# Feed-forward activations turned by VectorE block transposes and a round trip through memory

## The chip, the core and the metric

One core of a Trainium2 chip runs the whole program. TensorE multiplies matrices (its weight loads, PEld, run beside its matmuls), VectorE (DVE) and ScalarE (ACT) work on tiles element by element, GpSimd (POOL) does a few side tasks, and SyncE (SP) issues nearly all memory transfers; the 16 DMA engines of the core carry them out. The metric is the device time of one execution in microseconds. Three runs of the kernel before gave 1258.07, 1259.29 and 1259.97 us: the median is 1259.29.

## What is computed

One layer of a hybrid trunk over 256 tokens of width 2048, in float32. Two mixers (an RWKV-7 recurrence and a gated delta rule) stand ahead of the part that matters here, the feed-forward:

```python
h = rms_norm(x, ffn_norm_w[l])
x = x + (jax.nn.silu(h @ ffn_w_gate[l]) * (h @ ffn_w_up[l])) @ ffn_w_down[l]
return rms_norm(x, final_norm_w)
```

The hidden width is 5632. All three matrices are read once from memory, 138 MB in float32.

## The kernel before, in words

**Split products.** Every float32 operand is split in two float32r parts, high and low; a product is high x high, low x high and high x low, three matmuls of one pass each. Weights come as loads of 512 KB into `raw` (three buffers); ScalarE copies the high part to `wh` in two halves (line 197) and VectorE subtracts it from `raw` to give `wl` (line 198). `wh` and `wl` have two buffers each. `load_split` (line 172) does this for one load. I call one load and the twelve 512-wide matmuls that it feeds a part.

**The feed-forward** goes over 11 units of 512 hidden columns. For a unit, `gate` and `up` (lines 1071 and 1080, both through `gate_up`, line 1044) each take eight parts, with matmuls at line 1065, and give `sg`, two tiles of 128 tokens x 512 columns: ScalarE takes the silu (line 1076), VectorE multiplies by the `up` product (line 1084). `down` (line 1129) multiplies by `w_dn` in two halves `hf` of four parts each, matmuls at line 1142, and adds into `acc` (line 1150).

**The turn.** `down` needs the activations with hidden columns on partitions, but `sg` has tokens there. `turn` (line 1087) transposes `sg` on TensorE, eight 128x128 transposes (line 1097) into two PSUM banks, and ScalarE and VectorE split these into `h` (lines 241 and 242). The loop (from line 1168) takes the gate of the next unit, the first half of `down` of this one, `up` of the next, and the second half of `down`; in the middle of that half, after its second part, stands the turn of the next unit. The first unit's turn is called straight after its `up`, as there is no `down` before it; the scheduler puts it into the second unit's gate.

**Order.** A scheduler orders each engine's instructions by readiness and priority; loads and splits have high priority, so they run ahead as far as buffers allow. SP issues its transfers strictly in the order given, and each takes the next of eight completion semaphores in turn (DMAHW0 to DMAHW7), so that an issue has to wait until the transfer eight issues before it has landed. In unit 36, the last but one, five loads of the last unit's `w_dn` (`raw_end`, line 1057) stand among the others, through a single buffer; three more were loaded earlier.

Of the kernel before, what the change touches and what calls it, by code (L numbers as in the profile page):

```python
# [9 lines left out]
F32 = mybir.dt.float32  # L10
BF16 = mybir.dt.bfloat16
I32 = mybir.dt.int32
F32R = mybir.dt.float32r
# [4 lines left out]
P = 128  # L18
T = 256
# [30 lines left out]
def trunk_kernel(ctx, tc, xT, vecs, fnw, w_up, a_up, g_up, w_in, w_ab, w_out, w_gu, w_dn, out):  # L50
# [9 lines left out]
    def hi():  # L60
        return tc.high_priority(offset=HI)
# [11 lines left out]
    def mps(name, tag="mr"):  # L73
        return pm.tile([P, 512], F32, tag=tag, name=name)
# [22 lines left out]
    for r in range(2):  # L97
        rows = slice(64 * r, 64 * r + 64)
# [68 lines left out]
            assert any([g.step() for g in list(side)])  # L167


    first = []  # L170

    def load_split(src, by_k=False, whole=False):

        with hi():
            if first:
                raw = first.pop(0)
            else:
                raw = wp.tile([P, 1024], F32, tag="raw", name="raw", bufs=RAW)
                SY.dma_start(out=raw.rearrange("p (c f) -> p c f", c=4) if by_k else raw, in_=src)
            wh = wp.tile([P, 1024], F32R, tag="wh", name="wh", bufs=WH)  # L180
            wl = wp.tile([P, 1024], F32R, tag="wl", name="wl", bufs=WL)
            both = [(wh[:, h * 512:h * 512 + 512], wl[:, h * 512:h * 512 + 512]) for h in range(2)]
            if whole:
                split(wh, wl, raw)
                return both
            it = iter(both)
            return halves_of(raw, lambda: next(it), by_k)
# [856 lines left out]
    def gate_up(c0, m, tag="pb", beside=None):  # L1044

        banks = [pm.tile([P, 512], F32, tag=tag, name="psq") for _ in range(2)]
        b = c0 + 2 * m - NFB + 8
        ends = [(x % 4, x // 4) for x in (b, b + 1, b + 4, b + 5)] if 0 <= b < 4 else []
        for q in range(2):
            for kk in range(4):  # L1050
                if ends and kk % 2:
                    wend[ends[2 * q + kk // 2]] = halves_of(raw, own)
                elif ends:
                    raw = rp.tile([P, 1024], F32, tag="i1", name="raw_end")
                    i_, hf = ends[2 * q + kk // 2]
                    with hi():
                        SY.dma_start(out=raw, in_=w_dn[NFB - 4 + i_, hf])
                parts = load_split(w_gu[c0:c0 + 4, m, q, :, kk * 256:kk * 256 + 256].rearrange("c p f -> p c f"), True)
                for kx in range(2):
                    k = 8 * q + 2 * kk + kx  # L1060
                    t, ri = x2k[k]
                    wh, wl = parts[kx]
                    for o, w in ((0, wh), (T, wh), (0, wl)):
                        for tb in range(2):
                            last = PE.matmul(banks[tb], t[:, ri, o + tb * P:o + tb * P + P], w,  # L1065
                                             start=(k == 0 and o == 0 and w is wh), stop=(k == KB - 1 and w is wl))
                if beside and kk % 2:
                    beside(2 * q + kk // 2, last)
        return banks

    def gate(c0, beside=None):
# [15 lines left out]
    def turn(c0, sg, before=()):  # L1087
# [14 lines left out]
                split(h[:, hs, 0:T], h[:, hs, T:], p3)  # L1102
        return h

    nbank = [0]

    def wend_slots():

        one = ["lw", "SB", "sq2", "bk", "i3"] + ["kt", "rt"] * 2 + ["vt"] * 4
        bufs = {"kt": 2, "rt": 2, "vt": 4}  # L1110

        def places():
            x2w = rp.tile([P, 8, 512], F32R, tag="AT1", name="wend")
            for i in range(8):
                yield x2w[:, i, :]
            w = act.tile([P, 4, 2 * T], F32R, tag="act", name="wend")
            for i in range(4):
                yield w[:, i, :]
            w = rp.tile([P, 2, 512], F32R, tag="Yt", name="wend")
            yield w[:, 0, :]  # L1120
            yield w[:, 1, :]
            for t in one:
                yield rp.tile([P, 512], F32R, tag=t, name="wend", bufs=bufs.get(t, 1))
            for i in range(6):
                yield fp.tile([P, 512], F32R, tag=("wend", "sq2")[i // 4], name="wend", bufs=(4, 2)[i // 4])
        g = places()
        return lambda: (next(g), next(g))
# [26 lines left out]

    def turn_x2(i, before):

        tb, ps = i // 2, [mps("ps_xn", t) for t in ("mr", "mc")]
        q0 = i % 2 * 2
        ms = [PE.transpose(ps[q][:, k * P:k * P + P], x2[:, 4 * (q0 + q) + k, tb * P:tb * P + P], ident)
              for q in range(2) for k in range(4)]  # L1160
        together([before] + ms)
        for q in range(2):
            S.copy(acc[:, tb, (q0 + q) * 512:(q0 + q) * 512 + 512], ps[q])

    sg = gate(units[0], turn_x2)
    h = turn(units[0], up(units[0], sg, "mg"))

    for c, c1 in zip(units, units[1:]):
        sg = gate(c1)
        down(c, h, 0)  # L1170
        up(c1, sg)
        ahead = []
        down(c, h, 1, lambda m: ahead.append(turn(c1, sg, [m])))
        h = ahead[0]


    n = 4
# [110 lines left out]
```

## Time and profile before

| | |
|---|---|
| median of three runs | 1259.29 us |
| profiled execution, its own time | 1257.04 us |
| its span | 1255.3 us |
| TensorE clock granted | 0.998 |
| TensorE busy | 1231.5 us |
| VectorE / ScalarE busy | 835.0 / 650.4 us |
| transposes at line 1097 | 88, 11.4 us in all |
| bytes moved | 226.68 MB, 175701 packets, 181 GB/s |

In the page's groups, a line gives the source line, the engine, what is written from what, the count, the busy time in us and the mean in ns, and behind the second bar the idle time just before these instructions and what ended it. The chain is the sequence of work that ended last, each piece with its start and length. In timelines, a bracket gives the idle time before a piece and what released it.

### The profile page before, as it was taken

Reading aid. Unit: us, or ns where it says so; the run is one execution under the profiler, and the core shown is the slowest. Engines: PE = TensorE matmul, PEld = TensorE weight load, DVE = VectorE, ACT = ScalarE, POOL = GpSimd, SP = SyncE. Lnnn points to the kernel's source line nnn. Section 1 sums busy time; section 2 is a strip of 40 time slices with the busy share of each in tenths; the row PEclk is TensorE's granted clock in tenths of the full one; section 3 lists DMA queues with packets and bytes.
Section 4 is the critical chain, followed back from the end, with each engine's and each line's share of the span. In section 5 each row is a group of like instructions: output and inputs, shape, how many; then the busy total and the mean of one; then the engine's idle time right before and its main releaser. Section 6 shows DMA issues by size and latency. Waiting matters only on the chain.

```text
span 1255.3 us, 21107 instructions
## 1 busy us (share of the span) xinstructions
PE 1231.5 (98%) x8122; PEld 1084.1 (86%) x8122; DVE 835.0 (67%) x1634; ACT 650.4 (52%) x1199; POOL 17.0 (1%) x63
## 2 busy tenths in 40 slices
PE   7999999999999999999999999999999999999997
PEld 6999999999999989888888888888888888878886
DVE  7987887978966867555556555655656565665554
ACT  6665555666545556664444444444444444454443
POOL 3000000000000000000000000000000000000000
PEclk9999999999999999999999999999999999999999
DMA  6555666575573445676666666766666766676651
GB/s 232 167 168 178 162 170 157 168 183 142 179 231 118 135 165 188 167 209 191 190 191 195 188 190 194 197 188 197 186 187 189 194 187 195 202 239 192 194 150 67
DMA packets 175701, 226.68 MB, mean 181 GB/s; under 512 B 52272, under 2 KB 144560, under 8 KB 175344
## 3 DMA queue, kind: packets, MB, share of 16 engines
q1 hardware_dynamic: 171328, 222.19, 60.7%
q10 hardware_dynamic: 4128, 2.10, 0.6%
q8 instruction: 64, 1.05, 0.4%
q0 software_dynamic: 144, 1.05, 0.2%
q14 instruction: 37, 0.30, 0.1%
HBM read 218.75 MB, written 4.46 MB: 178 GB/s over the span
## 4 chain that ended last, share of the span: by engine, by line
PE 86%; DMA 5%; DVE 5%; ACT 1%; SPq 1%; issue 1%; DVEq 0%; ACTq 0%
PE psq L1065 36%; PE psd L1142 17%; PE psb L215 16%; PE psb L218 8%; DMA raw_end<-in_w_dn 2%; DVE wl L242 1%; PE psT L1097 1%; DMA raw<-in_w_in 1%; DMA A_r<-sA 1%; DMA sA<-AT 1%; PE psd L1193 1%; PE psd L1191 1%; PE psd L1192 1%; PE ps_A L480 1%; DVE wend L198 1%
## 5 line engine op out<-in xcount | busy, mean ns | idle before, releaser
L198 DVE TENSOR_TENSOR wl<-raw,wh 128x512 fp32r<-128x512 f32 x524 | 341.5, 694 | 273.0 <-ACT wh L197 271.0
L197 ACT ACTIVATE wh<-raw 128x512 fp32r<-128x512 f32 x524 | 302.0, 625 | 363.2 <-PE psq L1065 203.9
L1065 PE MATMUL psq<-wh,x2s 128*128 128x512 f32 x1408 | 377.4, 390 | 0.4 <-ACT wh L197 0.4
L1065 PEld LDWEIGHTS psq<-wh,x2s 128*128 128x128 f32 x1408 | 263.7, 188 | 55.6 <-ACT wh L197 1.0
L1065 PE MATMUL psq<-wl,x2s 128*128 128x512 f32 x704 | 217.2, 389 | 0.0
L215 PE MATMUL psb<-xs,wh 128*128 128x256 f32 x816 | 207.3, 288 | 7.6 <-ACT wh L197 6.1
L218 PE MATMUL psb<-xs,wh 128*128 128x256 f32 x816 | 206.9, 287 | 0.0
L1142 PE MATMUL psd<-wh,h 128*128 128x512 f32 x640 | 203.5, 391 | 1.0 <-ACT wh L197 1.0
L241 ACT ACTIVATE wh<-raw 128x1024 fp32r<-128x1024 f32 x128 | 135.3, 1057 | 86.6 <-PE psb L218 71.2
L215 PEld LDWEIGHTS psb<-xs,wh 128*128 128x128 f32 x816 | 157.3, 193 | 9.1 <-ACT wh L197 6.1
L242 DVE TENSOR_TENSOR wl<-raw,wh 128x1024 fp32r<-128x1024 f32 x128 | 155.9, 1218 | 10.8 <-ACT wh L241 10.7
L218 PEld LDWEIGHTS psb<-xs,wh 128*128 128x128 f32 x816 | 157.4, 193 | 1.5 <-issue 0.7
L1065 PEld LDWEIGHTS psq<-wl,x2s 128*128 128x128 f32 x704 | 132.0, 188 | 27.5
L1142 PEld LDWEIGHTS psd<-wh,h 128*128 128x128 f32 x640 | 119.1, 188 | 26.3 <-ACT wh L197 2.3
L215 PE MATMUL psb<-xs,wl 128*128 128x256 f32 x816 | 127.8, 287 | 2.2 <-DVE wl L198 1.2
L1142 PE MATMUL psd<-wl,h 128*128 128x512 f32 x320 | 124.6, 389 | 0.0
L215 PEld LDWEIGHTS psb<-xs,wl 128*128 128x128 f32 x816 | 110.4, 193 | 4.5 <-DVE wl L198 2.0
L1142 PEld LDWEIGHTS psd<-wl,h 128*128 128x128 f32 x320 | 60.1, 188 | 12.7
L218 PE MATMUL psb<-ys,wh 128*128 128x256 f32 x256 | 64.5, 288 | 2.5 <-DVE ys L242 2.5
L215 PE MATMUL psb<-ys,wh 128*128 128x256 f32 x256 | 64.7, 289 | 0.2 <-ACT ys L241 0.2
L218 PEld LDWEIGHTS psb<-ys,wh 128*128 128x128 f32 x256 | 50.1, 196 | 2.8 <-DVE ys L242 2.7
L1150 DVE TENSOR_TENSOR acc<-acc,psd 128x512 f32<-128x512 f32 x80 | 49.5, 681 | 1.8 <-PE psd L1142 1.8
(312 smaller groups left out, 1014.2 us busy)
## 6 DMA issues: line engine op xcount, KB each, us to landing
raw<-in_w_gu SPq DMA_DIRECT2D x176, 512.0 KB, 4.8
raw<-in_w_in SPq DMA_DIRECT2D x99, 512.0 KB, 3.9
raw<-in_w_dn SPq DMA_DIRECT2D x80, 512.0 KB, 4.2
raw<-in_w_out SPq DMA_DIRECT2D x32, 512.0 KB, 3.5
raw_end<-in_w_dn SPq DMA_DIRECT2D x8, 512.0 KB, 4.4
xraw<-in_xT SPq DMA_DIRECT2D x8, 256.0 KB, 6.3
x<-in_xT SPq DMA_DIRECT2D x1, 2048.0 KB, 9.7
raw<-in_w_ab SPq DMA_DIRECT2D x2, 512.0 KB, 6.1
```

Of the source, the lines that this page charges most:

```text
L197: S.activation(oh, src, AF.Copy)
L198: V.tensor_tensor(ol, src, oh, ALU.subtract)
L215: PE.matmul(ps[:, 0:T], w, rt[:, ri, 0:T], start=(first and k == 0 and not low), stop=(last and k == 7 and low == 1))
L218: PE.matmul(ps[:, 0:T], w, rt[:, ri, T:], start=False, stop=False)
L241: S.activation(hi_ap, src, AF.Copy)
L242: V.tensor_tensor(lo_ap, src, hi_ap, ALU.subtract)
L480: PE.matmul(psA[h][:, ch, :], bk[hr, ch].rearrange("p a t -> p (a t)"), ar[hr, p, ch].rearrange("p a t -> p (a t)"), start=True, stop=True)
L1065: last = PE.matmul(banks[tb], t[:, ri, o + tb * P:o + tb * P + P], w, start=(k == 0 and o == 0 and w is wh), stop=(k == KB - 1 and w is wl))
L1097: ms.append(PE.transpose(ps[b][:, o:o + P], sg[tb][:, (2 * b + i) * P:(2 * b + i) * P + P], ident))
L1142: m = PE.matmul(banks[tb * 2 + cg], st, parts[cg][w], start=(i == 0 and w == 0 and st is hh), stop=(i == n - 1 and st is hl))
L1150: V.tensor_tensor(acc[:, tb, cs], acc[:, tb, cs], banks[tb * 2 + cg], ALU.add)
L1191: PE.matmul(ps, hh, wh, start=(i == 0), stop=False)
```

## The change

Ten of the eleven turns leave TensorE. VectorE's block transpose turns each 32x32 block of `sg` in place (`tn0`, `tn1`, one for each 128 tokens). Eight writes then scatter these blocks to a tensor `sH` in memory, in pieces of 32 numbers (128 bytes), 512 pieces a write, and four reads bring them back as rows of 256 numbers (1 KB) on the partition of their hidden column, into the low half of the tile `h`. One ScalarE and one VectorE instruction then split the whole `h` (1024 numbers on each partition), where two of each split it from PSUM. The writes are called in the first two parts of the next gate, the reads in its fifth and sixth part, the split in its eighth; each group is tied behind the weight load that was issued last. Only the last unit keeps the turn on TensorE. The tile slot `i3`, now of `tn1`, is no longer among the places for the last `w_dn`. The transposes of `x2` stay where they were (the callback is now called in every part, and skips the even ones).

```diff
-                SY.dma_start(out=raw.rearrange("p (c f) -> p c f", c=4) if by_k else raw, in_=src)
+                loads.append(SY.dma_start(out=raw.rearrange("p (c f) -> p c f", c=4) if by_k else raw, in_=src))
...
-                if beside and kk % 2:
-                    beside(2 * q + kk // 2, last)
+                if beside:
+                    beside(4 * q + kk, last)
...
+    def turn_far(c0, sg):
+
+        tn = []
+        for tb in range(2):
+            tn.append(rp.tile([P, 512], F32, tag=("i2", "i3")[tb], name=f"tn{tb}"))
+            with hi():
+                V.transpose(tn[tb], sg[tb])
+        h = act.tile([P, 4, 2 * T], F32R, tag="act", name=f"h{c0}")
+        raw = h[:, :, T:].bitcast(F32)
+
+        sH = dr.tile([32, 16, 8, 32], F32, name=f"sH{c0}")
+        rows = sH.rearrange("r (i q) b c -> q r i (b c)", q=4)
+
+        def step(n, last):
+            with hi():
+                if n < 2:
+                    ds = [SY.dma_start(out=sH[:, :, 4 * n + a, :],
+                                       in_=tn[n][32 * a:32 * a + 32].rearrange("r (j c) -> r j c", c=32))
+                          for a in range(4)]
+                elif 4 <= n < 6:
+                    ds = [SY.dma_start(out=raw[32 * q:32 * q + 32], in_=rows[q]) for q in (2 * n - 8, 2 * n - 7)]
+                else:
+                    ds = []
+                if ds:
+                    together([loads[-1]] + ds)
+                if n == 7:
+                    split(h[:, :, 0:T], h[:, :, T:], raw)
+        return h, step
...
     sg = gate(units[0], turn_x2)
-    h = turn(units[0], up(units[0], sg, "mg"))
+    h, step = turn_far(units[0], up(units[0], sg, "mg"))
 
     for c, c1 in zip(units, units[1:]):
-        sg = gate(c1)
+        sg = gate(c1, step)
         down(c, h, 0)
         up(c1, sg)
-        ahead = []
-        down(c, h, 1, lambda m: ahead.append(turn(c1, sg, [m])))
-        h = ahead[0]
+        if c1 != units[-1]:
+            ahead = [turn_far(c1, sg)]
+            down(c, h, 1)
+        else:
+            ahead = []
+            down(c, h, 1, lambda m: ahead.append((turn(c1, sg, [m]), None)))
+        h, step = ahead[0]
```

On SP, the gate of the third unit before (its eight loads, each into a `raw` buffer; in brackets the semaphores waited for, where DVE is the buffer's last reader):

```order
L179 DMA raw_7675<-in_w_gu 128x4x256 [waits DMAHW6_49,DVE_49]
L179 DMA raw_7695<-in_w_gu 128x4x256 [waits DMAHW7_49,DVE_49]
L179 DMA raw_7715<-in_w_gu 128x4x256 [waits DMAHW0_49,DVE_49]
L179 DMA raw_7735<-in_w_gu 128x4x256 [waits DMAHW1_49,DVE_49]
L179 DMA raw_7755<-in_w_gu 128x4x256 [waits DMAHW2_49,DVE_49]
L179 DMA raw_7775<-in_w_gu 128x4x256 [waits DMAHW3_49,DVE_49]
L179 DMA raw_7795<-in_w_gu 128x4x256 [waits DMAHW4_49,DVE_49]
L179 DMA raw_7815<-in_w_gu 128x4x256 [waits DMAHW5_49,DVE_49]
```

The same gate now, up to its sixth load:

```order
L179 DMA raw_7671<-in_w_gu 128x4x256 [waits DMAHW2_49,DVE_49]
L1121 DMA sH4_7580<-tn0_7575 512x1x32 x3
L179 DMA raw_7695<-in_w_gu 128x4x256 [waits DMAHW3_49,DVE_49]
L1121 DMA sH4_7580<-tn0_7575 512x1x32
L1121 DMA sH4_7580<-tn1_7577 512x1x32
L1121 DMA sH4_7580<-tn1_7577 512x1x32 [waits DMAHW4_49]
L1121 DMA sH4_7580<-tn1_7577 512x1x32 [waits DMAHW5_49]
L179 DMA raw_7719<-in_w_gu 128x4x256 [waits DMAHW6_49,DVE_49]
L1121 DMA sH4_7580<-tn1_7577 512x1x32 [waits DMAHW7_49]
L179 DMA raw_7739<-in_w_gu 128x4x256 [waits DMAHW0_49,DVE_49]
L179 DMA raw_7759<-in_w_gu 128x4x256 [waits DMAHW1_49,DVE_49]
L1125 DMA h4_7579<-sH4_7580 32x4x256 [waits DMAHW4_49,DMAHW5_49,DMAHW3_49,DMAHW7_49,DMAHW2_49,PE_49]
```

Three writes stand behind the first load, four behind the second, one behind the third; the first read, behind the fifth load, waits for the landing of the writes. Behind these rows come the second read, the sixth load, two more reads, and the last two loads.

In the gate of the second unit, before, SP has loads alone:

```order
L179 DMA raw_7214<-in_w_gu 128x4x256 [waits DMAHW1_49,DVE_49]
L179 DMA raw_7234<-in_w_gu 128x4x256 [waits DMAHW2_49,DVE_49]
L179 DMA raw_7254<-in_w_gu 128x4x256 [waits DMAHW3_49,DVE_49]
L179 DMA raw_7274<-in_w_gu 128x4x256 [waits DMAHW7_49,DMAHW4_49,DVE_49]
L179 DMA raw_7294<-in_w_gu 128x4x256 [waits DMAHW5_49,DVE_49]
```

Now all eight writes stand behind its fourth load and wait for VectorE:

```order
L179 DMA raw_7213<-in_w_gu 128x4x256 [waits DMAHW1_49,DVE_49]
L1121 DMA sH0_7142<-tn0_7137 512x1x32 [waits DVE_49]
L1121 DMA sH0_7142<-tn0_7137 512x1x32
L1121 DMA sH0_7142<-tn0_7137 512x1x32 [waits DMAHW7_49]
L1121 DMA sH0_7142<-tn0_7137 512x1x32
L1121 DMA sH0_7142<-tn1_7139 512x1x32 [waits DVE_49]
L1121 DMA sH0_7142<-tn1_7139 512x1x32 [waits DMAHW2_49]
L1121 DMA sH0_7142<-tn1_7139 512x1x32 [waits DMAHW3_49]
L1121 DMA sH0_7142<-tn1_7139 512x1x32 [waits DMAHW4_49]
L179 DMA raw_7233<-in_w_gu 128x4x256 [waits DMAHW5_49,Activation_49]
```

The load of the fifth part (`raw_7233`) has moved behind the eight writes.

On VectorE, the end of the second unit's `up` before (`sg` products, then `wl` halves of the next `down` parts, then the splits of the turned `h4`):

```order
L1084 SCALAR_TENSOR_TENSOR sg_7314<-psq_7406,rstd2_6748,sg_7314 128x512
L1084 SCALAR_TENSOR_TENSOR sg_7315<-psq_7407,rstd2_6748,sg_7315 128x512
L198 TENSOR_TENSOR wl_7597<-raw_7594,wh_7596 128x512 x2
L198 TENSOR_TENSOR wl_7632<-raw_7629,wh_7631 128x512 x2
L198 TENSOR_TENSOR wl_7652<-raw_7649,wh_7651 128x512 x2
L242 TENSOR_TENSOR h4_7614<-psT_7615,h4_7614 128x2x256
L242 TENSOR_TENSOR h4_7614<-psT_7620,h4_7614 128x2x256
```

The same place now:

```order
L1084 SCALAR_TENSOR_TENSOR sg_7319<-psq_7411,rstd2_6748,sg_7319 128x512
L1084 SCALAR_TENSOR_TENSOR sg_7320<-psq_7412,rstd2_6748,sg_7320 128x512
L198 TENSOR_TENSOR wl_7608<-raw_7605,wh_7607 128x512
L1111 STREAM_TRANSPOSE tn0_7575<-sg_7319 128x512
L198 TENSOR_TENSOR wl_7608<-raw_7605,wh_7607 128x512
L1111 STREAM_TRANSPOSE tn1_7577<-sg_7320 128x512
L198 TENSOR_TENSOR wl_7628<-raw_7625,wh_7627 128x512 x2
```

The two transposes stand around the second half of one `wl`, and the splits of `h4` have left this place: they now follow the split of the next gate's fifth load, on ScalarE and VectorE alike (in the second unit's gate, that of the seventh).

More of the change, by code (lines that the diff above doesn't have):

```diff
@@ L167, in drain @@
             assert any([g.step() for g in list(side)])
-    first = []
+    first, loads = [], []
     def load_split(src, by_k=False, whole=False):
@@ L1103, in turn @@
         return h
+    def turn_far(c0, sg):
[23 more added lines that the diff above has]
+        return h, step
     nbank = [0]
     def wend_slots():
-        one = ["lw", "SB", "sq2", "bk", "i3"] + ["kt", "rt"] * 2 + ["vt"] * 4
+        one = ["lw", "SB", "sq2", "bk"] + ["kt", "rt"] * 2 + ["vt"] * 4
         bufs = {"kt": 2, "rt": 2, "vt": 4}
@@ L1155, in turn_x2 @@
     def turn_x2(i, before):
+        if i % 2 == 0:
+            return
+        i //= 2
         tb, ps = i // 2, [mps("ps_xn", t) for t in ("mr", "mc")]
```

## The prediction

> **What bounds the kernel now.** I read the page first, for the busy engine, the chain that ended last and the idle time of the groups.
>
> ```profile
> PE 1231.5 (98%) x8122; PEld 1084.1 (86%) x8122; DVE 835.0 (67%) x1634; ACT 650.4 (52%) x1199; POOL 17.0 (1%) x63
> ...
> L1065 PE MATMUL psq<-wh,x2s 128*128 128x512 f32 x1408 | 377.4, 390 | 0.4 <-ACT wh L197 0.4
> ...
> L1142 PE MATMUL psd<-wh,h 128*128 128x512 f32 x640 | 203.5, 391 | 1.0 <-ACT wh L197 1.0
> ```
>
> TensorE is busy 98% of the span, and in the feed-forward (lines 1065 and 1142) it is idle for 1.4 us in all. What is taken off TensorE there is time gained; what is added elsewhere costs only if TensorE has to wait for it. The chain in order of time gives the beat (start, length, what):
>
> ```profile
> 593.41 21.76 PE psq L1065 x96
> 615.17 5.44 PE psd L1142 x24
> 620.62 0.87 PE psT L1097 x8
> 621.49 5.47 PE psd L1142 x24
> 626.96 21.76 PE psq L1065 x96
> 648.72 10.88 PE psd L1142 x48
> 659.60 21.76 PE psq L1065 x96
> ```
>
> A unit is 66.19 us (593.41 to 659.60): 24 parts of twelve matmuls, 21.76 / 8 = 2.72 us each, which is 65.28, and 0.91 for the turn (0.87 for eight transposes, 0.03 in the block behind them, which takes 5.47 instead of 5.44). One 512 KB load feeds each part.
>
> How late may a load be? The timeline of ScalarE and of VectorE around one load, the DMA issues of 615 to 681 us (KB each, us to landing), and the list of waits (us in total, times, longest) say it.
>
> ```profile
> 672.79 1.16 ACT L197 ACTIVATE wh<-raw 128x512 fp32r<-128x512 f32 x2 [1.56 <-PE psq L1065]
> ...
> 680.95 1.16 ACT L197 ACTIVATE wh<-raw 128x512 fp32r<-128x512 f32 x2 [1.56 <-PE psq L1065]
> ```
>
> ```profile
> 673.65 1.29 DVE L198 TENSOR_TENSOR wl<-raw,wh 128x512 fp32r<-128x512 f32 x2 [1.62 <-ACT wh L197]
> ```
>
> ```profile
> raw<-in_w_gu SPq DMA_DIRECT2D x16, 512.0 KB, 5.0
> ```
>
> ```profile
> ACT wh L197 <- DMA raw<-in_w_gu: 24.0, 11, 3.4
> ```
>
> A load is issued when VectorE ends the split three parts before it (673.65 + 1.29 = 674.94), and its own split starts at 680.95: 6.0 us, of which landing takes 5.0. So 1.0 us of lateness moves nothing. Beyond it ScalarE starts late, and TensorE still has the 2.72 us of the part before, less 0.6 for the first half of the split: 2.1 us more. A load may be about 3.1 us late. The waits agree: ScalarE waited eleven times for a gate load, 2.2 us on average, and TensorE lost 1.4 us to it at lines 1065 and 1142 together.
>
> **The change, part by part.**
>
> *Off TensorE.* Ten of eleven turns go, by the rows above 10 x 0.91 = 9.1 us. Their splits from PSUM go too, on engines that wait anyway.
>
> *On VectorE.* Two block transposes of 128x512 per unit, put after both products of `sg` and around one `wl`.
>
> ```profile
> L364 DVE STREAM_TRANSPOSE tn_r<-st_r x2: 445/446/446, 187.0 to 271.8; 128x256 f32<-128x256 f32 x2
> ```
>
> ```profile
> 681.17 1.41 DVE L1084 SCALAR_TENSOR_TENSOR sg<-psq,rstd,sg 128x512 f32<-128x512 f32 x2 [0.99 <-PE psq L1065]
> 682.50 1.28 DVE L198 TENSOR_TENSOR wl<-raw,wh 128x512 fp32r<-128x512 f32 x2
> ```
>
> ```profile
> 681.20 1.07 PE L1142 MATMUL psd<-wh,h 128*128 128x512 f32 x4
> ```
>
> A 128x256 transpose took 446 ns (min, median, max in the tile's view), so a 128x512 one is between 0.45 (a size that costs nothing) and 0.89 us (twice); I take 0.8, near the double. The second `wl` half then ends at 682.5 + 0.65 + 0.8 + 0.65 = 684.6 instead of 683.8. TensorE begins that part at 681.20 + 2.72 = 683.9 and in its order uses this half from the ninth matmul, 1.8 us in, 685.7. Cost nothing; the cover is these 1.1 us, and without it each 0.1 us is 1 us in ten units. The next load goes 0.8 us later, within the 3.1.
>
> *In the queue.* Per unit eight writes of 64 KB in 128-byte packets (512 each, 4096 in all) and four reads of 128 KB in 1 KB packets (512 in all).
>
> ```profile
> q1 hardware_dynamic: 9593, 12.56, 67.5%
> ```
>
> ```profile
> DMA packets 2129, 0.79 MB, mean 199 GB/s; under 512 B 1996, under 2 KB 1996, under 8 KB 2129
> ...
> q1 hardware_dynamic: 2129, 0.79, 86.9%
> ```
>
> ```profile
> sA<-AT SPq DMA_DIRECT2D x8, 128.0 KB, 3.6
> ...
> sX_r<-X_r SPq DMA_DIRECT2D x4, 128.0 KB, 5.0
> ...
> TTg<-sX_g SPq DMA_DIRECT2D x4, 64.0 KB, 3.4
> ```
>
> ```profile
> L870 SPq DMA_DIRECT2D TTg<-sX_g x4: 486/488/900, 363.6 to 365.6; - x4
> ```
>
> These are the queue's totals from 615 to 681 us and from 178.6 to 182.6 us (packets, MB, share of 16 engines), three kinds of small transfers (KB each, us to landing), and the issue times of one. The first is one unit: 67.5% of 16 engines for 66 us is 713 us for 12.56 MB, or 57 us per MB; a load of 0.524 MB is 29.8 / 16 = 1.86 us, a 1 KB packet 58 ns. In the second the RWKV part writes its inverses to memory in 128-byte packets: 86.9% of 16 x 4.0 is 55.6 us, less 133 packets of 4 KB at 0.23 us (31 us), leaves 25 us for 1996, 12 ns each; 26 ns would be the bound with every packet alike. I take 15 ns: a write is 512 x 15 / 16 = 0.48 us, eight are 3.8; the reads 512 x 58 / 16 = 1.9. Together 5.7 us of a unit in which the engines idle 0.325 x 66 = 21 us. They do come in a burst. Three writes follow the first gate load, four the second, one the third. Against a beat of 2.72 the backlog is 1.86 + 3 x 0.48 - 2.72 = 0.6, then 1.86 + 4 x 0.48 - 2.72 = 1.1 more: the third load lands 1.6 us late, of 3.1 allowed. SP's time fits too: a 512-packet issue of the same shape took 0.49, so four and a load are some 2.3 us of 2.72. Cost nothing.
>
> *The reads and the split of `h`.* SP is in order, and the first read waits for all eight writes; the loads of parts 5 to 7 queue behind it. Parts of a gate are counted from 0, times from the issue of the first gate load. The last write goes at about 6.3 (behind the third load, 5.44), and lands 3.4 to 5.0 us after it by the rows, 1.2 later by the backlog left: 10.9 to 12.5, in the middle 11.7. The reads are due behind the fifth load, at 11.3: up to 1.2 us late. The last two go behind the sixth load, at 14.4, and land by 18.4 (4.0, the middle of these rows). ScalarE takes the split of `h` between those of parts 4 and 5:
>
> ```profile
> L241 ACT ACTIVATE wh<-raw 128x1024 fp32r<-128x1024 f32 x128 | 135.3, 1057 | 86.6 <-PE psb L218 71.2
> ...
> L242 DVE TENSOR_TENSOR wl<-raw,wh 128x1024 fp32r<-128x1024 f32 x128 | 155.9, 1218 | 10.8 <-ACT wh L241 10.7
> ```
>
> At this size they took 1.06 and 1.22. ScalarE ends at 19.5, VectorE at 20.7, the first `wl` half of part 5 at 21.4. TensorE starts part 5 at 22.4 and needs it four matmuls later, 23.3. The cover is 1.9 us, and the writes may be that much later than I put them. Cost nothing.
>
> *The first unit* has no `down` between its `up` and the next gate.
>
> ```profile
> 559.68 1.41 DVE L1084 SCALAR_TENSOR_TENSOR sg<-psq,rstd,sg 128x512 f32<-128x512 f32 x2 [0.15 <-PE psq L1065]
> 561.01 1.28 DVE L198 TENSOR_TENSOR wl<-raw,wh 128x512 fp32r<-128x512 f32 x2
> ```
>
> ```profile
> 568.52 1.15 ACT L197 ACTIVATE wh<-raw 128x512 fp32r<-128x512 f32 x2 [1.56 <-PE psq L1065]
> ```
>
> All eight writes stand on SP ahead of the load of part 4. The first transpose ends at 561.0 + 0.65 + 0.8 = 562.5; eight issues at 0.49 end at 566.4; the load goes at about 567, as its completion slot is that of the first write, and lands at 572. Its split would start at 568.52 - 0.91 = 567.6. Late by 4.4, less the 2.1 that TensorE has: 2.3. I take 2 us; 1 if the queue is quicker, 4 if the transfers behind the burst are slow.
>
> *The end loads* of unit 36 come two or three loads later, five as before.
>
> ```profile
> 1056.72 21.76 PE psq L1065 x96
> ...
> 1125.56 0.45 PE psq L1065 x2
> ```
>
> That unit took 68.84, 2.65 over the beat; I add 0.3, between -1 and +2.
>
> Sum: -9.1 + 2.0 + 0.3 = -6.8. The profiled execution took 1257.04 us (span 1255.3), so it would take 1250.2; the median of the runs stands 2.25 higher, at 1259.29, and my number on that scale is 1252.5.
>
> **A rule that speaks against it.** The trace shows 128-byte packets at 12 to 26 ns. The Trainium skill's page "DMA: Bandwidth & Descriptors", section "Specifications", asks for at least 512 B per transfer and says that below this the engine does a read-modify-write. By that rule, a write packet costing about twice what the trace's smallest reading gives, the estimate would be the second rival's and not the forecast's; the rows just above do not show it, but they hold only 1996 such packets, for 4 us.
>
> **The rivals.**
>
> *Late writes eat the gain.* The eight completion slots of SP and the wait for all writes act together. If a write lands after 6.8 us instead of 4.2, the reads are 2.6 + 0.4 late, TensorE waits 3.0 - 1.9 = 1.1 us in each of nine units, 10 us: -6.8 + 10 = 1262; at 6.3 us it is 5 us and 1258. For it: the 5.0 us row was measured with only two writes in flight. Against: 3.4 and 3.6. I price it at no change, 1259.3.
>
> *Slow small packets: slower.* Place: the second gate load of each unit, and the reads. At 30 ns (a bit over the bound of 26) a write is 0.96; the backlog is 1.86 + 2.88 - 2.72 = 2.0, then 1.86 + 3.84 - 2.72 = 3.0 more: the third load 5.0 late, 1.9 past its cover, and the last write lands at 6.3 + 4.2 + 5.0 = 15.5 instead of 11.3, so that the reads are 4.2 late, 2.3 past theirs. The two overlap: 2.3 us in nine units, 21, and 4 instead of 2 in the first: 1259.3 - 9.1 + 21 + 4 + 0.3 = 1275. It decides from 7 x w - 2.3 > 3.1, w = 0.77 us per write, 24 ns; between lie 1260 to 1275. For it: the destination rows lie 1 KB apart and the source is 32 partitions. Against: the 12 ns.
>
> *The gain is not there.* If the transposes take 1.5 us and not 0.8, `wl` comes 0.3 us past its cover, and with the load behind it 0.4 us of each 0.91 is paid back: -9.1 + 4 + 2.3, 1256.5.
>
> **How the numbers follow.** A measurement of this kernel tells 0.2%, 2.5 us. Forecast 0.56, its own range 1250 to 1255; late writes 0.14 (1257 to 1262); slow packets 0.25 (1260 to 1275); gain not there 0.05, which lies on the edge: I count 0.03 as faster, 0.02 as same. Of the late writes 0.03 are slower, 0.01 faster, 0.10 same. Faster 0.60, same 0.12, slower 0.28. The range goes from 1249.5, below which would be more than all turns, to 1268, the middle of the slow packets: about 0.14 left out above, 0.03 below.
>
> **What would show it.** Right: no TensorE idle before line 1065 at the sixth gate part, units of 65.3 us in the chain, one gap of 1 to 3 us in the first unit; packets up by 46,000 and DMA share in a unit near 76%; writes landing in 4 to 5 us. Wrong: ScalarE's split of `h` waiting for the reads, or loads of gate parts 2, 3 and 5 with a long wait on SP and TensorE idle behind them in every unit.

## The result, and the profile after

The kernel with the change takes 1309.67 us (median of four runs, 1308.01 to 1311.06); the kernel before, run beside it on the same chip, takes 1259.63 (1258.07 to 1260.76). The ratio is 1.0405 with a 95% interval of 1.0387 to 1.0422: slower by 50 us, where 7 us faster was forecast. The range ended at 1268. Ratios here and below leave out two single executions far above the others (2024 us of one kernel below, 4307 us of the kernel before).

The profiled execution has a span of 1306.3 us, 51.0 more than before. The page of the kernel after, its line of busy times and the group of the gate and `up` matmuls, says where they are:

```profile
PE 1244.3 (95%) x8042; PEld 1083.7 (83%) x8042; DVE 844.5 (65%) x1644; ACT 648.5 (50%) x1189; POOL 17.0 (1%) x63
...
L1065 PE MATMUL psq<-wh,x2s 128*128 128x512 f32 x1408 | 389.8, 399 | 37.4 <-ACT wh L197 37.4
```

TensorE is idle for 37.4 us ahead of these matmuls, each time until ScalarE's split of a weight; before it was 0.4. And although 80 transposes are gone, TensorE is busy 12.8 us longer: the same 1408 matmuls have a mean of 399 ns instead of 390. The idle time added here and the busy time added, 37.0 + 12.8, are 49.8 of the 51.

The chain of the kernel after, in order of time, shows one unit (start, length, what; short pieces left out):

```profile
599.47 21.76 PE psq L1065 x96
621.23 8.17 PE psd L1171 x36
...
631.81 5.95 DMA raw<-in_w_gu
...
640.86 7.68 DMA h<-sH
...
648.65 1.06 ACT h L241
...
651.62 9.16 PE psq L1065 x32
660.79 10.88 PE psd L1171 x48
```

The chain leaves TensorE twice: to the third gate load, and to the last read of `h`. A unit that was 66.19 us, and that should have become 65.28, is 72.2 (the chain's next `up` begins at 671.67). The nine beats between the starts of the `up` streams have a mean of 71.5 us. The gaps are in the timeline of TensorE (in brackets the idle time before a piece and what ended it):

```profile
638.55 1.20 PE L1065 MATMUL psq<-wh,x2s 128*128 128x512 f32 x4 [1.00 <-ACT wh L197]
...
650.28 1.20 PE L1065 MATMUL psq<-wh,x2s 128*128 128x512 f32 x4 [3.28 <-ACT wh L197]
```

The timeline of ScalarE names what stands behind the second one:

```profile
643.02 1.15 ACT L197 ACTIVATE wh<-raw 128x512 fp32r<-128x512 f32 x2 [1.63 <-DMA raw<-in_w_gu]
648.65 1.06 ACT L241 ACTIVATE h<-h 128x1024 fp32r<-128x1024 f32 x1 [4.48 <-DMA h<-sH]
649.61 2.17 ACT L197 ACTIVATE wh<-raw 128x512 fp32r<-128x512 f32 x4
```

ScalarE is through with gate part 4 at 644.2 and waits 4.48 us for the reads, with the weights of part 5 behind it in its order. SP's timeline gives the times of the way through memory:

```profile
624.27 0.38 SPq L179 DMA_DIRECT2D raw<-in_w_gu  x1
624.70 1.94 SPq L1121 DMA_DIRECT2D sH<-tn  x3
626.74 1.26 SPq L179 DMA_DIRECT2D raw<-in_w_gu  x1
628.04 3.67 SPq L1121 DMA_DIRECT2D sH<-tn  x4
631.81 0.95 SPq L179 DMA_DIRECT2D raw<-in_w_gu  x1
632.80 0.56 SPq L1121 DMA_DIRECT2D sH<-tn  x1
633.46 1.95 SPq L179 DMA_DIRECT2D raw<-in_w_gu  x2
638.21 1.22 SPq L1125 DMA_DIRECT2D h<-sH  x2
...
640.27 1.18 SPq L1125 DMA_DIRECT2D h<-sH  x2
```

Against the first gate load at 624.27, the third load goes at 7.5 (forecast 5.44), the first read at 13.9 (11.3), the last two at 16.0 and 16.6 (by 14.4), and that read has landed at 640.86 + 7.68 = 648.54, at 24.3 (18.4). Between the fifth load (through at 635.41) and the first read (638.21) SP issues nothing. The list of SP's waits for the whole run says why (us in total, times, longest):

```profile
SPq L1125 <- DMA sH<-tn: 22.9, 9, 2.7
```

In nine of the ten units SP waits some 2.5 us for a write to land before it may issue the first read. The page's DMA issues have the landing of both kinds (KB each, median us), and the view of the tile `tn` the issue time of the writes and the transposes (ns, min/median/max):

```profile
sH<-tn SPq DMA_DIRECT2D x80, 64.0 KB, 4.6
...
h<-sH SPq DMA_DIRECT2D x40, 128.0 KB, 6.7
```

```profile
L1121 SPq DMA_DIRECT2D sH<-tn x80: 555/630/1615, 562.1 to 1205.0; - x80
L1111 DVE STREAM_TRANSPOSE tn<-sg x20: 702/705/708, 561.4 to 1196.2; 128x512 f32<-128x512 f32 x20
```

A write lands about as fast as forecast (4.6 us for 4.2), but the last one goes at 8.5 instead of 6.3, and the first read waits for it. The reads land more slowly than forecast (6.7 to 7.7 for 4.0). The rest of the unit's loss is in the windows behind the second gap (start:end, length, busy time of the five engines, granted clock, DMA share, GB/s; the middle row lies inside the first):

```profile
650.20:656.00 5.80, 5.58 (x16) 4.15 (x17) 3.81 (x7) 2.74 (x6) 0.00 (x0) 0.71 0.45 126
651.80:655.20 3.40, 3.40 (x9) 2.63 (x10) 1.57 (x3) 0.75 (x2) 0.00 (x0) 0.50 0.59 165
656.00:660.00 4.00, 4.00 (x20) 3.27 (x19) 1.95 (x4) 1.15 (x2) 0.00 (x0) 1.00 0.62 218
```

Over the 5.8 us behind the wait TensorE's granted clock is 0.71 on average, though there is work; it is 0.50 from 651.8 to 655.2 us, which costs half of these 3.4 us, 1.7. From 650.28 to 660.62 TensorE does three parts, 8.16 us at full clock, in 10.3. So a unit is 65.28 + 1.0 + 3.3 + 2.2 = 71.8, and the measured 72.2 is nearly explained.

### The profile page after: what moved, and what is told of

Read it like the earlier page. It is cut to its first block, busy times and chain, and to the rows that moved or that the text cites. A ratio compares the mean times of both kernels' runs of the same rounds, so it can differ in the third digit from the quotient of the medians.

```text
span 1306.3 us, 21155 instructions
## 1 busy us (share of the span) xinstructions
PE 1244.3 (95%) x8042; PEld 1083.7 (83%) x8042; DVE 844.5 (65%) x1644; ACT 648.5 (50%) x1189; POOL 17.0 (1%) x63
## 4 chain that ended last, share of the span: by engine, by line
PE 68%; DMA 15%; DVE 10%; ACT 3%; issue 2%; SPq 2%; ACTq 0%; DVEq 0%
PE psq L1065 25%; PE psd L1171 14%; PE psb L215 14%; PE psb L218 7%; DMA h<-sH 5%; DMA raw<-in_w_gu 4%; DVE wl L198 3%; DVE wl L242 2%; DMA raw<-in_w_in 1%; DMA raw_end<-in_w_dn 1%; ACT wh L197 1%; ACT h L241 1%; PE ps_A L480 1%; DVE wend L198 1%; PE psd L1229 1%
## 5 line engine op out<-in xcount | busy, mean ns | idle before, releaser
L1065 PE MATMUL psq<-wh,x2s 128*128 128x512 f32 x1408 | 389.8, 399 | 37.4 <-ACT wh L197 37.4
L1065 PEld LDWEIGHTS psq<-wh,x2s 128*128 128x128 f32 x1408 | 269.6, 193 | 103.2 <-ACT wh L197 46.7
L1065 PE MATMUL psq<-wl,x2s 128*128 128x512 f32 x704 | 224.5, 400 | 1.7 <-DVE wl L198 0.5
L1171 PE MATMUL psd<-wh,h 128*128 128x512 f32 x640 | 200.5, 389 | 0.0
L241 ACT ACTIVATE wh<-raw 128x1024 fp32r<-128x1024 f32 x128 | 135.2, 1056 | 87.6 <-PE psb L218 69.7
L242 DVE TENSOR_TENSOR wl<-raw,wh 128x1024 fp32r<-128x1024 f32 x128 | 156.1, 1220 | 11.4 <-ACT wh L241 11.2
L1065 PEld LDWEIGHTS psq<-wl,x2s 128*128 128x128 f32 x704 | 134.8, 193 | 33.8 <-DVE wl L198 5.6
L218 PEld LDWEIGHTS psb<-ys,wh 128*128 128x128 f32 x256 | 50.2, 196 | 2.8 <-DVE ys L242 2.7
L215 PEld LDWEIGHTS psb<-ys,wh 128*128 128x128 f32 x256 | 50.1, 196 | 0.9 <-ACT ys L241 0.4
```

Of the source, the lines that this page charges most:

```text
L215: PE.matmul(ps[:, 0:T], w, rt[:, ri, 0:T], start=(first and k == 0 and not low), stop=(last and k == 7 and low == 1))
L218: PE.matmul(ps[:, 0:T], w, rt[:, ri, T:], start=False, stop=False)
L241: S.activation(hi_ap, src, AF.Copy)
L242: V.tensor_tensor(lo_ap, src, hi_ap, ALU.subtract)
L1171: m = PE.matmul(banks[tb * 2 + cg], st, parts[cg][w], start=(i == 0 and w == 0 and st is hh), stop=(i == n - 1 and st is hl))
```

## The experiments

The theories. **A**: the reads come late, and ScalarE, which works in order, holds the next weight split behind them. **B**: the burst of writes on the queue delays the loads. **C**: the reads, as transfers, slow the loads beside them, whoever waits for them. Beats are the times between the starts of two successive `up` streams in TensorE's timeline; "first segment" is the time from the first gate matmul to the first `up` matmul of the second unit (81.6 us before, 88.2 with the change). Where only one time is given, it is that of a single run, and the kernel before took 1256 to 1258 us on the same chip; its own runs there lie between 1253.7 and 1261.2, so differences of a few us between single times tell little, and the beats are read instead.

**Writes that nobody reads.** The turn stays on TensorE; beside it come the block transposes and the eight writes.

```diff
+    step = turn_far(units[0], sg)[1]
+    h = turn(units[0], sg)
...
+        sg = gate(c1, step)
```

> The turn stays on TensorE as before; the block transposes and the eight writes per unit are added, nobody reads what they write. Theory A (the reads come late and ScalarE, which is in order, waits for them ahead of a weight split): about 1275, which is before plus 5 in the first unit and 1 in each of nine, where a gate load is late behind the writes. Theory B (the burst of writes in the queue is the cause by itself): 1300 or more. Theory C (the reads are the cause as transfers, since they slow the loads beside them): 1265 to 1275.

Measured: 1265.74 us. The chain, in order of time:

```profile
598.33 21.76 PE psq L1065 x96
...
625.53 0.87 PE psT L1097 x8
...
664.51 21.76 PE psq L1065 x96
```

664.51 - 598.33 = 66.18, the beat of before, with all eight writes beside it: they cost nothing in these units. Of the 9 us more than the kernel before on that chip, 7 are in the first segment (84.8 for 81.6) and in the unit with the end loads (72.5 for 68.8). B falls for the other units. Theory A's own number, about 1275, was too high: it counted 1 us in each of nine units, and they lost nothing.

**Writes and reads that nobody waits for.** As that, with the four reads at their places, into a tile that nobody uses.

```diff
+                elif 4 <= n < 6:
+                    ds = [SY.dma_start(out=dead[32 * q:32 * q + 32], in_=rows[q]) for q in (2 * n - 8, 2 * n - 7)]
```

> As the run before, and the four reads per unit stand where the change has them, into a tile that nobody uses; the turn stays on TensorE. Theory A: 1275 to 1280, since no engine waits for the reads. Theory B: 1300 or more, as with the writes alone. Theory C: 1305 to 1320, the change's time and some 9 for the turns.

Measured: 1270.52 us, below the ranges of A (1275 to 1280) and of C. The beats are 66.3 to 67.5 outside the unit with the end loads, on average 0.7 over 66.19. The reads take as long as in the change, though no engine is held up by them:

```profile
dead<-sH SPq DMA_DIRECT2D x40, 128.0 KB, 6.8
```

So their lateness is not made by the stall, and as mere transfers they cost 0.7 us a unit with the turn on TensorE: C is true, and small.

**The split put last.** The change, with the split of `h` tied behind the gate's last weight split on ScalarE and VectorE.

```diff
-                    split(h[:, :, 0:T], h[:, :, T:], raw)
+                    a, b = splits[-1]
+                    together([a, S.activation(h[:, :, 0:T], raw, AF.Copy)])
+                    together([b, V.tensor_tensor(h[:, :, T:], raw, h[:, :, 0:T], ALU.subtract)])
```

> The change, with the split of h tied behind the gate's last weight split on ScalarE and on VectorE. Theory A: 1255 to 1270, because 3.3 us of idle TensorE and about 2.6 of lowered clock go in each of nine units. Theories B and C: 1295 or more, since the transfers are the same.

Measured: 1271.79 us, just past the 1270 that A allowed. The beats have a mean of 67.2, without the unit with the end loads (70.0); the page's group:

```profile
L1064 PE MATMUL psq<-wh,x2s 128*128 128x512 f32 x1408 | 382.2, 393 | 16.5 <-ACT wh L197 16.3
```

No transfer changed, and 38 of the 50 us come back, out of idle time (37.4 to 16.5) and mean (399 to 393 ns). A holds for the larger part. What remains is 1.9 us a unit over 65.28, and comes of loads that are late: TensorE still waits for ScalarE's weight splits, and ScalarE for their loads (up to 4.1 us in the unit from 636 to 652 us).

**The split last, and one read of 4 KB rows** into 128 partitions in place of four of 1 KB rows into 32.

```diff
-        sH = dr.tile([32, 16, 8, 32], F32, name=f"sH{c0}")
+        sH = dr.tile([4, 32, 4, 8, 32], F32, name=f"sH{c0}")
...
+                    ds = [SY.dma_start(out=raw, in_=sH.rearrange("q r i b c -> (q r) i (b c)"))]
```

> The late split, and sH laid out so that one read of 512 KB in rows of 4 KB to all 128 partitions replaces the four reads of 1 KB rows to 32 partitions each. Theory A: as the late split, within 5. Theory B: 1290 or more. Theory C: clearly under the late split, by 15 or more, since the read then is a load like those of the weights.

Measured: 1268.85 us, beats of 66.9 on average without the unit with the end loads, landing of the one read 8.1 us. That is 0.3 us a unit less than with four reads; the form of the reads is not what the loss hangs on.

**The same read, with the split where the change has it.** Only `sH`, the writes' places in it and the read are edited.

```diff
-                elif 4 <= n < 6:
-                    ds = [SY.dma_start(out=raw[32 * q:32 * q + 32], in_=rows[q]) for q in (2 * n - 8, 2 * n - 7)]
+                elif n == 4:
+                    ds = [SY.dma_start(out=raw, in_=sH.rearrange("q r i b c -> (q r) i (b c)"))]
```

> The change with one read of 4 KB rows into 128 partitions in place of the four reads of 1 KB rows into 32 partitions, in the order of the change, with the split of h where the change has it. One issue of 0.57 us takes the place of four with loads between them, so the read starts 2 to 3 us before the last of the four did. If it lands within 6 to 8 us, TensorE's idle time goes from 4.3 us a unit to 1 or 2, and beats are 66.5 to 68.5 us. If the memory way itself is late whatever the form of the reads: 70 us or more.

Measured: 1296.73 us, beats 68.8 to 71.3, mean 70.0: 1.5 us a unit better than the change, but over the 66.5 to 68.5 expected; by the expectation's other case (70 us or more) the way through memory is late whatever the form of the reads. One unit on ScalarE:

```profile
642.70 1.15 ACT L197 ACTIVATE wh<-raw 128x512 fp32r<-128x512 f32 x2 [4.02 <-DMA raw<-in_w_gu]
646.46 1.06 ACT L241 ACTIVATE h<-h 128x1024 fp32r<-128x1024 f32 x1 [2.60 <-DMA h<-sH]
```

The one read is issued 12.2 us after that unit's first gate load (638.61 and 626.39 on SP) and has landed at 20.0, four sooner than in the change; ScalarE still waits 2.6 us for it. It now waits 4.0 us for the load ahead as well: from 630 to 650 us the first queue is busy for 91.7%, and loads land after 6.6 us. The wait for the reads is shorter, and part of it is handed to the loads.

**Reads without writes.** Only the first unit writes; all ten read the first unit's activations, and the writes of the other nine are left out.

```diff
-                if n < 2:
+                if n < 2 and c0 == units[0]:
```

> The change without the writes of the later units: only the first unit writes its turned activations, and all ten units read those, at the same places of the order (the later units compute with the first unit's activations). What it tells apart is why the reads are late. If the eight issues of the writes and the load that they hold up are the whole of it, the reads are back where the prediction had them and beats are 65.3 to 65.9 us. If reads into 32 partitions beside loads land after 6.7 us or more whatever is ahead of them, about half stays: issued some 3 us earlier they still land 2 to 3 us behind the 18.4 of the prediction, and beats are 66.5 to 69 us. If the reads alone do it all: 71 us as in the change.

Measured: 1290.76 us, mean beat 69.7. The DMA issues:

```profile
h<-sH SPq DMA_DIRECT2D x40, 128.0 KB, 7.6
```

This lies between the two last cases of the expectation. SP's timeline shows the gate of the third unit:

```profile
622.60 11.10 SPq L179 DMA_DIRECT2D raw<-in_w_gu  x5
633.76 1.19 SPq L1129 DMA_DIRECT2D h<-sH  x2
...
635.62 1.20 SPq L1129 DMA_DIRECT2D h<-sH  x2
```

Counted from the first gate load at 622.60, the first read now goes at 11.2 and the last two from 13.0, no later than the forecast 11.3 and 14.4, and still TensorE waits. Of the 6.2 us that a unit of the change loses against 65.28, 4.5 remain without any write ahead of the reads, and 1.7 go. The landing of the reads is the larger cause; the writes and their issue are the smaller. The two parts need not add up exactly, as the reads land after 7.6 us here and after 6.7 in the change.

**The stall alone.** The kernel before, with no new transfer: twelve copies of a constant on ScalarE between the splits of the fifth and the sixth gate part.

```diff
+        if n == 4:
+            stall[:] = [S.copy(scr, wbc[:, 0:512]) for _ in range(12)]
+            together([splits[-1]] + stall)
+        elif n == 5:
+            together([stall[-1], splits[-2], splits[-1]])
```

> The kernel before, with its turn on TensorE and no transfer added, but with twelve copies of 128x512 on ScalarE (0.63 us each, 7.5 us in all, of constants into a scratch tile that nobody reads) between the weight splits of the fifth and the sixth gate part, where the change has its wait for the reads. The prediction's slack there is 1.9 us plus the 1.06 us of the split, so TensorE should idle some 4.5 us a unit, as in the change. If the lower granted clock behind the wait comes of TensorE's idling alone, the matmuls behind it run slow here too, and beats are 72 to 74 us (idle 4.5, slow matmuls 2 to 3). If it comes of the transfers: the granted clock stays at 1.00 there and beats are 70.0 to 71.5 us.

Measured: 1315.95 us, beats of 71.7 (78.1 in the unit with the end loads), between the two ranges expected, as TensorE idles 3.6 us a unit and not 4.5. What decides is the clock. The timeline of TensorE, and the windows behind the gap (clock and DMA share are the two numbers before the last):

```profile
936.65 1.85 PE L1065 MATMUL psq<-wh,x2s 128*128 128x512 f32 x4 [3.56 <-ACT wh L197]
```

```profile
935.00:939.00 4.00, 2.35 (x6) 1.89 (x7) 2.37 (x4) 3.13 (x6) 0.00 (x0) 0.74 0.06 8
939.00:943.00 4.00, 4.00 (x16) 3.19 (x16) 1.42 (x3) 1.15 (x2) 0.00 (x0) 0.83 0.78 247
```

A wait on ScalarE at this place makes such a unit without any transfer: 3.56 us idle, and 71.7 - 66.19 - 3.56 = 1.9 us more in slow matmuls. The clock is down where the DMA share is 0.06, so transfers beside it are not needed to lower it.

**The first unit's turn left on TensorE**, the rest as in the change.

```diff
-    h, step = turn_far(units[0], up(units[0], sg, "mg"))
+    h, step = turn(units[0], up(units[0], sg, "mg")), None
```

> The change with one turn alone, that of the first unit, left on TensorE as before. The first unit's segment, from the first gate matmul to the first up matmul, takes 88.2 us in the change and 81.6 in the kernel before. If the first unit's share of the loss is its own (its eight writes and four reads stand on the queue right ahead of its gate loads): 82 to 83 us for the segment and 1302 to 1305 us in all. If the queue only moves the loss on to the next unit: no less than 1307.

Measured: 1302.18 us, first segment 82.0, later beats 71.4 as in the change. So the first unit's way through memory takes about 6 us more than its turn on TensorE (88.2 - 82.0). The forecast had 2 us less the 0.9 of the turn, 1.1.

**Another order of a unit, as a control.** Gate, `up`, then both halves of `down`, all turns on TensorE; with two pairs of PSUM banks in turn.

```diff
-        sg = gate(c1)
-        down(c, h, 0)
-        up(c1, sg)
+        sg = gate(c1, None, X[0])
+        up(c1, sg, X[1])
+        down(c, h, 0, Y)
```

> Control for the next two kernels: the turn stays on TensorE as in the kernel before, and only the order of a unit is another one: gate, up, and then both halves of the down product of the unit before, so that the sixteen weight parts of gate and up come first. Both theories expect the time of the kernel before, 1256 to 1262 us, unit beats of 66 to 66.5 us and no idle time of TensorE at L1065 beyond that of before. If the two long runs of down matmuls without a load between them starve the weight stream, it shows here and not in the change: beats over 67.

Measured: 1259.43 us (10 runs) beside 1257.8 for the kernel before, ratio 1.0019 (1.0003 to 1.0036). Two beats at a time, in the chain:

```profile
630.77 43.52 PE psq L1064 x192
...
690.62 0.87 PE psT L1095 x8
...
696.96 43.52 PE psq L1064 x192
```

A unit takes 66.19, as before: with the turn on TensorE, the order itself gives nothing.

**That order with the change spread out.** The gate and `up` streams are sixteen parts on end here, so the writes go singly behind eight loads (from the fourth part), the reads behind the thirteenth and fourteenth, and the split of `h` behind the last weight split.

```diff
+                if 3 <= n < 11:
+                    a, b = (n - 3) % 4, n - 3
+                    ds = [SY.dma_start(out=sH[:, :, b, :],
...
+                elif 12 <= n < 14:
...
+                if n == 15:
```

> That order with the change's way through memory, its transfers spread: one write behind each of eight weight loads, two reads behind each of two later loads, and the split of h put behind the last weight split of gate and up, so that no weight split stands behind it on ScalarE. Theory A (the reads come late and ScalarE, which works in order, holds the next weight split back behind them): nothing waits for the reads any more, beats of 65.3 to 65.9 us, and 1249 to 1255 us in all, faster than the order's control by 4 to 9 us of the 9.1 that ten turns hold on TensorE, less what the first unit gives back. Theory C (the transfers slow the loads beside them whatever waits for them): beats of 66 to 67, about the control's time or over it. Theory B (the burst of eight writes is what delays the loads): as theory A, since the burst is gone.

Measured: 1253.59 us, ratio 0.9961 (0.9946 to 0.9976). One unit of its chain:

```profile
625.17 43.52 PE psq L1064 x192
668.69 21.76 PE psd L1169 x96
690.45 43.52 PE psq L1064 x192
```

65.28 to the hundredth: 24 parts and no turn. The reads land after 7.1 us, as late as ever, and nobody waits. This is the gain that the prediction had in mind, 0.91 a unit, and it needed the waits moved. Against the kernel with the split put last, 67.2 a unit, two things differ, the order of a unit and the spreading of the writes over it; these runs do not tell which of the two gave the last 1.9 us.

**The same with one read of 4 KB rows.** The writes also begin one part later, from the fifth part, and go to other places of `sH`.

```diff
-                elif 12 <= n < 14:
-                    ds = [SY.dma_start(out=raw[32 * q:32 * q + 32], in_=rows[q]) for q in (2 * n - 24, 2 * n - 23)]
+                elif n == 13:
+                    ds = [SY.dma_start(out=raw, in_=sH.rearrange("q r i b c -> (q r) i (b c)"))]
```

> As the kernel with spread transfers, but laid out in memory so that one read of 4 KB rows into all 128 partitions takes the place of four reads of 1 KB rows into 32 partitions each. Theory C in the form that reads into 32 partitions slow the loads: 2 to 6 us less than with four reads. Theory A: within 2 us of it, 1249 to 1255 us, since nothing waits for the reads in either.

Measured: 1250.5 us, ratio 0.9935 (0.9912 to 0.9957), faster than both the kernel before and the change. Beats are 65.28 here too, so the 3 us between the two kernels are not from the steady units, and their intervals overlap.

**The end loads spread over two units.** In the last two kernels one unit, with end loads of the last `w_dn` among its transfers, takes 71.0 to 71.8 instead of 65.28 (the two beats around it 136.29 in the kernel with one read). Here each of the eight end loads is tied behind every fourth part over two units, and so is its split.

```diff
+                        together([loads[-1], SY.dma_start(out=raw, in_=w_dn[NFB - 4 + i_, hf])])
```

> The kernel with the other order of a unit and one read of 4 KB rows, whose beats were 65.28 us in all units but one: the unit with six of the eight end loads, 71.0 us. Here the eight end loads are spread over two units, one behind every fourth part, each tied to its place, and so are their splits. If those loads are what that unit lost 5.7 us by: beats of 65.3 to 66.5 us in both units, and 1244 to 1248 us in all. If the order or the turn costs it: 1249 to 1252 as before.

Measured: 1250.43 us, ratio 0.9947 (0.9928 to 0.9965): no gain. The two units now take 138.67 for 130.56. Eight end loads in them lose 8.1 us, where five (not six, as the expectation has it) lost 5.7 in one unit; about 1 us each, on average, though TensorE does not stand still by equal pieces. The places that the split end loads go to are also taken in another order. The expectation missed, and why an extra load costs 1 us with the transfers beside it stays open.

## Why the prediction was wrong

**The step that failed** is "the reads and the split of `h`", priced "Cost nothing" against a cover of 1.9 us. It let the last two reads go by 14.4 and land by 18.4, "4.0, the middle of these rows". They went at 16.0 and 16.6 and had landed at 24.3, 5.9 us late. The forecast cover of 1.9 was that of VectorE's `wl`; TensorE in fact waited for ScalarE's `wh`, where the same figures give 22.4 - (19.5 + 0.6) = 2.3. That leaves 3.6, less the 0.3 by which TensorE itself came later (650.28 - 3.28 - 624.27 = 22.7 for 22.4): 3.3, and 3.28 was measured. That TensorE came so nearly when forecast is luck: without the turn it needs part 5 some 0.9 us earlier, and the 1.0 us lost to the third load put that back. The mechanism that would hurt was named under "what would show it": ScalarE's split of `h` waiting for the reads. Two terms were mis-sized. The larger is the landing, 6.7 to 7.7 us for 4.0; the smaller is the time of issue, 1.6 to 2.6 us later, because the last write went late. The rows that gave 4.0 come from another part of the kernel, the RWKV mixer. The first queue while the reads of the unit above are in flight, 638.2 to 648.6 us (packets, MB, share of 16 engines):

```profile
q1 hardware_dynamic: 2519, 2.45, 101.0%
```

It has no idle time left, and it moves less than forecast: 101.0% of 16 x 10.4 us for 2.45 MB is 69 us per MB, where the prediction took 57 and spread the reads over the idle time of a whole unit. Why a MB costs more there, and why transfers in the mixer landed sooner, stays open: the queue was full there at times as well (100.6% from 185 to 192 us of the kernel before, where reads of 64 KB landed after 4.3 us). Late loads and the burst of writes are not needed for it, as the reads without writes land no sooner. That kernel kept 4.5 of the 6.2 us a unit, and the split put last gave back 38 of the 50 us.

**A term was missing:** the clock. Behind the wait TensorE has 3.4 us at a clock of 0.50, 1.7 us more in eight of the nine units between `up` streams. The prediction counted only idle time.

**Off TensorE**, 0.91 a turn: right. 66.19 against 65.28 in two kernels with the same order.

**On VectorE**, 0.8 us a transpose at no cost: right in effect (0.705 us), and in the spread kernels the beat has no room for any cost.

**In the queue**: half right. The eight writes hide whole in the beat when nothing waits for the reads. Their price per packet can be worked out from the page's first queue (packets, MB, share of 16 engines) in the kernel with unread writes,

```profile
q1 hardware_dynamic: 213568, 227.43, 62.8%
```

and in the kernel before,

```profile
q1 hardware_dynamic: 171328, 222.19, 60.7%
```

62.8% of 16 x 1264.0 less 60.7% of 16 x 1255.3 is 509 us for 42240 more packets, about 12 ns each; 15 was taken. The Trainium skill's page "DMA: Bandwidth & Descriptors", section "Specifications", asks for at least 512 B because of a read-modify-write below that. These 128-byte writes do not show a doubled price. The factor of two was the prediction's own reading, as that section gives no price. The rival's threshold was also added up wrongly: the backlog is 7 x w - 2 x (2.72 - 1.86) = 7 x w - 1.7, so it decides from w = 0.69 us, 21 to 22 ns, and not 24; at 12 ns that changes nothing. The issue was off, 0.63 us a write for 0.49: the third load went 2.1 us late and landed after 5.95, and in the change TensorE idled 1.0 us for it, past the 3.1 allowed. With the turn still on TensorE the same lateness cost nothing, as the turn lies between the unit's first gate load and its first gate matmul (8.6 us from SP's to TensorE's timeline in the kernel with unread writes, 7.7 in the change): taking the turn away also brings the need for the next loads some 0.9 us forward.

**The first unit**, 2 us (1 to 4): too small. Against its turn on TensorE it lost about 6, so by the sum's own account, with the 0.9 of the turn, about 7. TensorE's timeline there:

```profile
575.09 2.08 PE L1065 MATMUL psq<-wh,x2s 128*128 128x512 f32 x4 [4.92 <-ACT wh L197]
```

4.92 us idle, and the four matmuls behind take 2.08 instead of 1.07. The load of part 4 (the chain's 567.55, forecast "about 567") landed after 6.75 and not after 5.

**The end loads**, +0.3: not seen in the change, where that unit took 72.1 like the others; in the other order it is 5.7 to 6.5 us over its beat, 2.9 in the control.

**The rivals.** A write landed neither late (4.6 us, not 6.8) nor from slow packets, so neither of these two came true by its mechanism, though both had the right place: reads late past their cover. What the late writes were to do, send the first read 3 us late, did come about (2.6 us), but from the eight issues, and it is the smaller part of the loss. The doubt was put on the writes, and the landing of the reads was held at one value.

## What to carry to other kernels

Take the landing time of a new transfer from what lands at its own place, not from another part of the kernel: here the gate loads beside the reads took 5.0 us before and 5.5 with the change, the reads 6.7, and 4.0 was taken. Put the instruction that waits for a round trip behind all that its in-order engine owes the busiest one, and spread the transfers over the longest stretch of stream; the same transfers and the same split were 4% slower in the change and 0.4% faster in the other order, with the wait moved and the transfers spread; moving the wait alone gave back 38 of the 50 us, and what the spreading gives by itself was not measured. And price a wait of TensorE at more than its idle time.

## What was unexpected of the hardware

Behind gaps of 3.28 and 3.56 us TensorE's granted clock fell (0.71, 0.74 and 0.83 in the rows above, which are averages; over 3.4 us inside them, 651.8 to 655.2 and 936.9 to 940.3, it is 0.50 and 0.51). The length of the gap does not decide it alone: in the change the shortest beat, 69.3 us, is that of a unit whose gap of 2.30 us was followed by full clock (1.00 from 864.4 to 867.8), but in the kernel with reads and no writes a gap of 1.88 us was followed by 0.57 (0.51 from 717.2 to 720.6),

```profile
717.01 1.91 PE L1065 MATMUL psq<-wh,x2s 128*128 128x512 f32 x4 [1.88 <-ACT wh L197]
```

```profile
717.00:721.00 4.00, 3.98 (x11) 3.12 (x12) 3.11 (x5) 1.52 (x3) 0.00 (x0) 0.57 0.27 73
```

while in the kernel with writes and reads that nobody waits for one of 2.94 us was followed by full clock:

```profile
574.81 1.20 PE L1065 MATMUL psq<-wh,x2s 128*128 128x512 f32 x4 [2.94 <-ACT wh L197]
```

```profile
574.80:581.00 6.20, 5.82 (x24) 4.35 (x24) 2.57 (x4) 1.96 (x4) 0.00 (x0) 1.00 1.12 228
```

The Trainium skill's page "TensorE: Matmul & The Clock Gate", section "Part 1: The HAM clock gate (the "warmup" mystery)", says that the clock falls to half after an idle window of about 3.4 us; the drop and its size agree with the 0.50 here, the length as a threshold does not, since 1.88 us was enough once. What decides between gaps of the same length stays open.
